# The down projection of a SwiGLU trunk by seven products of halves, its factors made beside gate and up

## The chip, the cores and the metric

The kernel runs on one core of one Trainium2 chip, as one program and one launch. The metric is the time of an execution on the device in microseconds. The kernel before was timed three times: 2983.25 us median, 2979.05 to 2986.69.

## The reference

Two layers of one trunk are computed in fp32 for 1024 latent tokens and 256 context tokens of width 1024. Each layer has a mixer (three kinds of heads between one input and one output projection) and a SwiGLU FFN. Both are normed before and after and are modulated by a vector of the condition:

```python
h_lat = modulate(rmsnorm(x_lat, n1_pre[l]), mod_l[0], mod_l[1])          # the same for h_ctx
y_lat, y_ctx = hybrid_mixer(h_lat, h_ctx, ..., need_ctx)
x_lat = x_lat + mod_l[2] * rmsnorm(y_lat, n1_post[l])
f_lat = swiglu(modulate(rmsnorm(x_lat, n2_pre[l]), mod_l[3], mod_l[4]), ffn_w_gu[l], ffn_w_down[l])
x_lat = x_lat + mod_l[5] * rmsnorm(f_lat, n2_post[l])                    # x_ctx too, in layer 0 only

def swiglu(h, w_gu, w_down):
    g, u = jnp.split(h @ w_gu, 2, axis=-1)
    return (jax.nn.silu(g) * u) @ w_down
```

The FFN is 2816 wide: `w_gu` is 1024 x 5632, `w_down` 2816 x 1024. The context of the last layer has no FFN. The modulation vectors are products of the condition with `mod_w`, six of 1024 a layer.

## The kernel before

Tokens come in ten tiles of 128: 0 and 1 are the context, 2 to 9 the latents. The hidden units of the FFN come in 22 chunks of 128. Every fp32 operand of a large product is split in two fp32r parts, high and low: `halve` lets ScalarE make the high part by a cast and VectorE the low part by a subtraction. `mm3` (L325) then issues three matmuls, high by high, high by low and low by high.

A layer is a row of stages: input projection, mixers, output projection, gate and up of the latents, gate and up of the context (layer 0 only), down. In the profiled execution, in us from the span's start, gate and up of layer 0 run from 758 to 1240, the context's from 1240 to 1372, down to 1703; the projection of layer 1 follows. Gate and up of layer 1 end at 2722, down at 2965, the program at 2978.5.

Gate and up of the latents (class `Up`) already go by seven products for each chunk. The left factors a11, a12, a22 and s1 to s4 are quarters of the latents' normed activations, and sums of quarters; they are made once and stay. The right factors b11, b21, b22 and t1 to t4 are quarters of a chunk's gate and up weights and their differences: `diff` makes the t on GpSimd, `prepare` halves all seven. A chunk has 84 matmuls of 128x512. `head` runs the first two products, `tail` the other five, and between them the results are copied out of the accumulators by ScalarE (L210, L226, L229) or added by VectorE (L213, L242, L249). Silu of gate times up is made on GpSimd (L250, L260), and GpSimd issues the stores to `gd`, four of 128 rows of 2 KB a chunk (L221). The context's 256 tokens follow in `up_context`, with one store of 128 rows a chunk.

Down (`down_stage`) loads `gd` and `w_down` again, halves both, and goes through two halves of five token tiles each (layer 1: of four). For each half the chunks come in groups of two or four. A group runs, for each tile, its chunks by two column halves by three matmuls of 128x512 (L1130) and adds the result to the sums `ya` (L1137). At the last group `post` norms each tile, multiplies by the gate, adds the residual and stores. In layer 0 the next projection's first five tiles are normed and transposed too (`normed`, L547 to L561): one after each group of the second half, the last one after the stage.

The order on each engine: instructions run in the order of their queue. That order is made by a scheduler from the order of emission, and `net.order(a, b)` fixes one pair. SyncE issues the loads. Beside the FFN of layer 0 the modulation vectors are made by VectorE: `mod_stream` yields pieces, each a few 128x512 multiply-adds to `macc` (L523, L525) over a weight tile `ms`. `paced` counts the cost that the main stream yields and advances `mod_stream` by one piece for every 5.6 (gate and up) or 5.2 (down) of it.

## Time and profile before

| | us |
|---|---|
| three runs, median (lowest to highest) | 2983.25 (2979.05 to 2986.69) |
| the profiled execution | 2980.31 |
| its span, first to last instruction | 2978.5 |
| TensorE busy | 2785.4 |
| VectorE busy | 1902.6 |
| ScalarE busy | 1353.1 |
| GpSimd busy | 705.9 |
| mean granted clock of TensorE | 0.965 of 2.4 GHz |

The profile is of one execution. Busy times are of an engine's own instructions. An engine that waits is shown with what ended its wait. A matmul record is longer than the distance to the next one, as matmuls overlap: so a price for a matmul is taken from a stretch's busy time divided by its count. Views used below: windows (busy time of each engine in a stretch), waits of one engine grouped by what ended them, lines (groups of instructions of one line and shape), and the timeline of an engine.

### The profile page before, as it was taken

How to read it: one execution, taken by the hardware profiler on the slowest of the kernel's cores; microseconds unless marked ns; L12 is line 12 of the kernel's file. 1: busy time of each engine (PE TensorE's matmuls, PEld its weight loads, DVE VectorE, ACT ScalarE, POOL GpSimd, SP SyncE). 2: the span in 40 equal slices, each digit the busy share in tenths (PEclk: the TensorE clock that was granted, in tenths of full speed). 3: DMA queues.
4: the chain of work that ended last, by engine and by line, in shares of the span. 5: the costliest groups of instructions: out<-in, count | busy, mean ns of one | idle time of the engine just before them, and what ended most of it. 6: DMA issues, size and time to landing. Idle time of an engine off the chain costs nothing. (4 is left out here: it accounts for less than half of the span.)

```text
span 2978.5 us, 43813 instructions
## 1 busy us (share of the span) xinstructions
PE 2785.4 (94%) x16296; PEld 2373.5 (80%) x16296; DVE 1902.6 (64%) x3640; ACT 1353.1 (45%) x2796; POOL 705.9 (24%) x596
## 2 busy tenths in 40 slices
PE   6999899979899989999999889999888999999998
PEld 4999788868677768898888789888776788887886
DVE  3465578866685994446888664788857443344565
ACT  4454577645433323444242255477645433334331
POOL 0000233310345445200000000043402555552000
PEclk8999789989999999999999999999988999999999
DMA  7743000065453432576665344200164322224552
GB/s 237 222 137 98 24 12 9 13 199 185 142 187 102 139 106 83 166 220 205 194 226 177 109 130 115 72 5 12 54 213 151 97 85 85 82 67 168 165 198 85
DMA packets 339809, 370.45 MB, mean 124 GB/s; under 512 B 45440, under 2 KB 261516, under 8 KB 339596
## 3 DMA queue, kind: packets, MB, share of 16 engines
q1 hardware_dynamic: 327100, 329.38, 35.7%
q0 software_dynamic: 11776, 35.66, 3.2%
q8 instruction: 128, 2.10, 0.3%
q10 hardware_dynamic: 720, 2.62, 0.2%
q14 instruction: 85, 0.70, 0.1%
HBM read 300.19 MB, written 67.40 MB: 123 GB/s over the span
## 5 line engine op out<-in xcount | busy, mean ns | idle before, releaser
L1130 PE MATMUL b<-wh,g 128*128 128x512 f32 x792 | 218.8, 394 | 9.2 <-ACT g L1458 6.9
L1130 PE MATMUL b<-dh,g 128*128 128x512 f32 x792 | 215.7, 390 | 2.6 <-DVE ya L1137 2.5
L326 PE MATMUL b<-wh,hh 128*128 128x256 f32 (+1 forms) x592 | 173.3, 294 | 21.8 <-DVE hh L560 20.7
L1130 PEld LDWEIGHTS b<-wh,g 128*128 128x128 f32 x792 | 149.2, 189 | 44.2 <-ACT g L1458 8.1
L1130 PEld LDWEIGHTS b<-dh,g 128*128 128x128 f32 x792 | 148.4, 188 | 35.4 <-DVE ya L1137 4.5
L525 DVE SCALAR_TENSOR_TENSOR macc<-ms,csil,macc 128x512 f32<-128x512 f32 x196 | 175.4, 935 | 0.9 <-DMA ms<-in_mod_w 0.9
L326 PE MATMUL b<-wh,hl 128*128 128x256 f32 (+1 forms) x592 | 171.4, 290 | 1.3 <-DVE hl L561 1.2
L634 DVE TENSOR_TENSOR wl<-ws,wh 128x1024 fp32r<-128x1024 f32 (+2 forms) x68 | 79.8, 1176 | 145.0 <-ACT wh L633 145.0
L326 PE MATMUL b<-wl,hh 128*128 128x256 f32 (+1 forms) x592 | 171.6, 290 | 0.5 <-DVE wl L634 0.5
L1137 DVE TENSOR_TENSOR ya<-ya,b 128x512 f32<-128x512 f32 x180 | 116.1, 681 | 84.0 <-PE b L1130 83.7
L326 PE MATMUL b<-hh,wh 128*128 128x320 f32 (+1 forms) x472 | 149.0, 316 | 0.0
L326 PE MATMUL b<-hl,wh 128*128 128x320 f32 (+1 forms) x472 | 147.2, 312 | 0.0
L326 PE MATMUL b<-hh,wl 128*128 128x320 f32 (+1 forms) x472 | 146.9, 311 | 0.0
L326 PEld LDWEIGHTS b<-wh,hh 128*128 128x128 f32 x592 | 114.3, 193 | 25.6 <-ACT code L692 17.2
L1056 DVE TENSOR_TENSOR ptl<-b,pth 128x640 fp32r<-128x640 f32 (+2 forms) x144 | 107.4, 746 | 34.5 <-ACT pth L1055 33.1
L633 ACT CAST wh<-ws 128x1024 fp32r<-128x1024 f32 (+2 forms) x68 | 68.7, 1012 | 128.3 <-PE b L326 89.2
L1055 ACT CAST pth<-b 128x640 fp32r<-128x640 f32 (+2 forms) x144 | 90.9, 631 | 76.0 <-PE b L1050 75.1
L1130 PE MATMUL b<-wl,g 128*128 128x512 f32 x396 | 123.8, 392 | 0.1
L1130 PE MATMUL b<-dl,g 128*128 128x512 f32 x396 | 122.4, 389 | 0.0
L1037 DVE CUSTOM_DVE_ANT_0 pe<-b,swm,sink 128x640 f32<-128x640 f32 (+1 forms) x128 | 108.0, 845 | 12.8 <-PE b L1032 12.3
L326 PEld LDWEIGHTS b<-wh,hl 128*128 128x128 f32 x592 | 114.3, 193 | 2.0 <-DVE hl L561 2.0
L326 PEld LDWEIGHTS b<-wl,hh 128*128 128x128 f32 x592 | 114.5, 193 | 0.7 <-DVE wl L634 0.7
(386 smaller groups left out, 8528.5 us busy)
## 6 DMA issues: line engine op xcount, KB each, us to landing
ws<-in_ffn_w_down SPq DMA_DIRECT2D x88, 512.0 KB, 4.0
ms<-in_mod_w SPq DMA_DIRECT2D x144, 256.0 KB, 3.2
rg<-in_ffn_w_gu SPq DMA_DIRECT2D x66, 512.0 KB, 4.0
ru<-in_ffn_w_gu SPq DMA_DIRECT2D x66, 512.0 KB, 3.8
ws<-in_w_in SPq DMA_DIRECT2D x56, 512.0 KB, 4.8
gd<-ct POOLq DMA_DIRECT2D x88, 256.0 KB, 2.9
gr<-gd SPq DMA_DIRECT2D x44, 320.0 KB, 4.0
gr<-gd SPq DMA_DIRECT2D x44, 256.0 KB, 3.8
```

The lines of the kernel that those rows point to most:

```text
L326: mm = lambda x, y, **kw: self.nc.tensor.matmul(out, x, y, skip_group_check=more, **kw)
L525: nc.vector.scalar_tensor_tensor(x, st, c, x, op0=ALU.mult, op1=ALU.add)
L633: nc.scalar.copy(h[:, : kk * nn], st[:, : kk * nn])
L634: nc.vector.tensor_sub(lo[:, : kk * nn], st[:, : kk * nn], h[:, : kk * nn].bitcast(F32))
L1037: nc.vector.tensor_tensor_reduce(out=p, in0=sc, in1=b["mask"], scale=1.0, scalar=sink, op0=ALU.add, op1=ALU.min, accum_out=mn)
L1055: nc.scalar.copy(hi, pv)
L1056: nc.vector.tensor_sub(lo, pv, hi.bitcast(F32))
L1130: nc.tensor.matmul(ps[n], x[:, s], y[:, n * 512 : (n + 1) * 512], start=(c == 0 and pi == 0), stop=(c == nk - 1 and pi == 2))
L1137: nc.vector.tensor_add(y, y, ps[n])
```

## The change

A product of two matrices of 2x2 blocks has eight products of blocks. The change computes down with seven, for each pair of token tiles: (0, 1) in layer 0, and (2, 6), (3, 7), (4, 8), (5, 9). The rows of a block matrix are the two tiles, the columns are the chunks c and c + 11; `w_down` is cut in the same rows and in its two column halves. So T = 5 pairs in layer 0, 4 in layer 1.

- Gate and up goes through its chunks in the order 0, 11, 1, 12, ... After the second of a pair, `factors` makes s1 to s4 from the four results (four operations, VectorE for the latents, GpSimd for the context) and stores seven factors to `gx`, each 128 rows by 4 tiles by 128 (the context: one tile). After the first of a pair, `differences` loads two chunks of `w_down`, makes four differences in place (two on VectorE, two on GpSimd) and stores them to `td`.
- `prepare` can be ordered after the copy of an accumulator, and t3, b22 and t4 of a chunk are halved in its own head.
- `down_stage` runs seven products p, each over all pairs t: a step (p, t) is 11 chunks by three matmuls into one accumulator. Results are added into `ya` and `yb`. Product 5 finishes the first tile of a pair, product 6 the second; from the second step of product 6 on two of the next projection's tiles are normed a step. A step costs 7.5 for `paced`, with 4.4 a piece.
- Staging of the modulation has four buffers beside gate and up in place of eight. In layer 0 the context's tile 1 is normed whole before the tails begin.

```diff
+    def factors(self, pool, j, w, vector):
+
+        nc = self.nc
+        g, at, n = self.g, self.lat if w == 512 else 0, w // P
+        v = lambda x: g[x][:, :w]
+        new = lambda x: g.setdefault(x, self.net.t(pool, f"g{x}", [P, w], bufs=1 if w == 512 else 2))
+        store = lambda x: nc.gpsimd.dma_start(self.gx[:, SUMS.index(x), at : at + n, j, :], v(x).rearrange("p (t n) -> p t n", n=P))
+        new("s1"), new("s2"), new("s4")
+        vector.tensor_add(v("s1"), v("s3"), v("a22"))
+        vector.tensor_sub(v("s2"), v("s1"), v("a11"))
+        vector.tensor_sub(v("s3"), v("a11"), v("s3"))
+        vector.tensor_sub(v("s4"), v("a12"), v("s2"))
+        for x in SUMS:
+            store(x)
+        g.clear()
+
+    def differences(self, pool, j):
+
+        nc, w = self.nc, self.net.a["ffn_w_down"]
+        t = self.net.t(pool, "td", [P, 4, 512], bufs=1)
+        for r in range(2):
+            c = j + KF * r
+            nc.sync.dma_start(t[:, 2 * r : 2 * r + 2, :].rearrange("p h n -> p (h n)"), w[self.l, c * P : (c + 1) * P, :])
+        b11, b12, b21, b22 = [t[:, x, :] for x in range(4)]
+        nc.vector.tensor_sub(b11, b12, b11)
+        nc.gpsimd.tensor_sub(b12, b22, b12)
+        nc.vector.tensor_sub(b22, b22, b11)
+        nc.gpsimd.tensor_sub(b21, b22, b21)
+        nc.sync.dma_start(self.td[:, :, j, :], t)
...
-    def prepare(self, c, x):
-        self.net.halve(*self.slot(c, x), self.raw[c, x])
+    def prepare(self, c, x, after=None):
+        r = self.net.halve(*self.slot(c, x), self.raw[c, x])
+        if after is not None:
+            self.net.order(r, after)
 
     def product(self, out, c, x, y, first=False):
...
         self.product(X, c, "b11", "a11", True)
         p1 = self.tmp()
-        nc.scalar.copy(p1, X)
+        copied = nc.scalar.copy(p1, X)
+        if c > 1:
+            for x in ("t3", "b22", "t4"):
+                self.prepare(c, x, copied)
         self.product(Y, c, "b21", "a12", True)
         g0 = self.tmp()
...
         p5 = self.tmp()
-        nc.scalar.copy(p5, Z)
+        copied = nc.scalar.copy(p5, Z)
         if 1 < n < NFC:
-            self.prepare(n, "b11")
-            self.prepare(n, "b21")
+            self.prepare(n, "b11", copied)
+            self.prepare(n, "b21", copied)
         if more:
             self.diff(n, "t1")
             self.diff(n, "t2")
@@ -241,27 +295,29 @@
...
+            self.prepare(n, "t1", freed)
+            self.prepare(n, "t2", freed)
         yield 2.7
         self.product(Z, c, "b22", "s4")
         c12 = self.tmp()
...
             self.diff(n, "t3")
-            self.prepare(n, "b22")
-            self.prepare(n, "t3")
         yield 2.7
         self.product(X, c, "t4", "a22")
         g1 = self.tmp()
         net.act(g1, X, AF.Silu)
-        nc.gpsimd.tensor_mul(g1, g1, c22)
-        store(768, g1)
+        nc.gpsimd.tensor_mul(mine(("s3", "a22")[r]), g1, c22)
         if more:
             self.diff(n, "t4")
-            self.prepare(n, "t4")
+        if n == 1:
+            for x in ("t3", "b22", "t4"):
+                self.prepare(1, x)
+        if r:
+            self.factors(self.sg, j, 512, nc.vector)
+        else:
+            self.differences(self.sg, j)
...
-                    if need_ctx:
-                        next(rest)
-                        for _ in range(8):
-                            next(st)
                     for _ in rest:
                         pass
-                with tp("mb", "left") as mb:
+
+                with tp("sg", "left") as up.sg:
+                    for x in SUMS:
+                        self.t(up.sg, f"g{x}", [P, 512], bufs=1)
+                    self.t(up.sg, "td", [P, 4, 512], bufs=1)
                     if need_ctx:
-
-                        self.mring = mb, 8
+                        self.mring = up.sg, 4
                         self.back = self.mod_stream("dve", [(0, 5)] + [(l + 1, j) for j in (1, 0, 2)])
                     self.paced(st, 5.6)
                     for _ in self.back:
@@ -1265,7 +1264,7 @@
             if need_ctx:
                 self.mring = dn, 3
                 self.back = self.mod_stream("dve", [(l + 1, j) for j in (3, 4, 5)])
-            self.paced(self.down_stage(l, dn, need_ctx, up.gd), 5.2)
+            self.paced(self.down_stage(l, dn, need_ctx, up), 4.4)
...
+    def down_stage(self, l, dn, need_ctx, up):
...
+        def weight(p, j):
+
+            c, n = 2 * j, min(2, KF - 2 * j)
+            if p % 2 and j < 5:
+                h, lo = [x.rearrange("p k t -> p (k t)")[:, j * D : (j + 1) * D] for x in self.H]
+            else:
+                pool, xs = (dn, ("dl", "dh")) if p % 2 == 0 and j < 4 else (self.wp, ("wl", "wh"))
+                lo, h = [self.t(pool, x, [P, D], F32R, bufs=4) for x in xs]
+            t = self.t(self.wp, "ws", [P, D], bufs=2)[:, : n * 512]
+            nc.sync.dma_start(t.rearrange("p (c n) -> p c n", c=n), source(p, c, n))
+            self.halve(h[:, : n * 512], lo[:, : n * 512], t)
+            return [(h[:, q * 512 : (q + 1) * 512], lo[:, q * 512 : (q + 1) * 512]) for q in range(n)]
+
+        def acts(p, t):
+            h, lo = [self.t(dn, f"a{x}", [P, KF, P], F32R, bufs=2) for x in "hl"]
+            for c0, c1 in ((0, 6), (6, KF)):
+                raw = self.t(dn, "ar", [P, 6, P], bufs=2)[:, : c1 - c0]
+                nc.sync.dma_start(raw, up.gx[:, p, t, c0:c1, :])
+                self.halve(h[:, c0:c1], lo[:, c0:c1], raw)
             return h, lo
 
...
+        lo_, hi_ = slice(0, 512), slice(512, D)
+        for n, (p, t) in enumerate(seq):
+            k = n - p * T
+            if k == 0:
+                cur, ahead = W.pop(), []
+            ah, al = nexta
+            if n + 1 < len(seq):
+                nexta = acts(*seq[n + 1])
+            if p < 6:
+                for j in range(6 * k // T, 6 * (k + 1) // T):
+                    ahead += weight(p + 1, j)
+            if k == T - 1:
+                W.append(ahead)
+            ps = self.b1()
+            for c in range(KF):
+                self.mm3(ps, ah[:, c, :], al[:, c, :], cur[c][0], cur[c][1], c == 0, c == KF - 1)
+            A0, A1, B0, B1 = ya[t][:, lo_], ya[t][:, hi_], yb[t][:, lo_], yb[t][:, hi_]
+            if p == 0:
+                nc.scalar.copy(B0, ps)
+            elif p == 1:
+                nc.vector.tensor_add(A0, B0, ps)
+                square(A0, half[:, t, 0:1])
+            elif p == 2:
+                nc.vector.tensor_add(B0, B0, ps)
+            elif p == 3:
+                nc.vector.tensor_add(A1, B0, ps)
+            elif p == 4:
+                nc.vector.tensor_add(B0, B0, ps)
+                nc.vector.tensor_add(B1, A1, ps)
+                square(B1, half[:, T + t, 0:1])
+            elif p == 5:
+                nc.vector.tensor_add(A1, A1, ps)
+                finish(pairs[t][0], ya[t], hi_, half[:, t, :], False)
+            else:
+                nc.vector.tensor_sub(B0, B0, ps)
+                finish(pairs[t][1], yb[t], lo_, half[:, T + t, :], final)
+                if k == 1 and nxt:
                     self.plan(l + 1)
-            cur = ahead
+                for _ in range(2 if k else 0):
+                    if nxt:
+                        nxt.pop(0)()
+            yield 7.5
         for f in nxt:
             f()
 
```

The context's changed chunk, in `up_context`, multiplies silu by up for each of the two tiles apart and calls `up.factors(cu, j, P, nc.gpsimd)` after the second chunk of a pair. `finish` takes the place of `post`: it sums the squares of the two halves of a row, and norms, multiplies and adds as before.

The order on TensorE at the start of gate and up of layer 0: head 1, then s2 by t2 of chunk 0 (names: left factor, right factor, each with h or l for its part; `ht` is the normed context tile 1, `ident` the identity for a transpose). Before:

```order
L326 MATMUL b_1568_8490<-s2h_7109,t2l_8467 128x512
L326 MATMUL b_1604_8646<-s1h_7111,t1h_8460 128x512
...
L326 MATMUL b_1604_8646<-s1h_7111,t1l_8461 128x512
L326 MATMUL b_1652_8892<-a11h_7105,b11h_8785 128x512
...
L326 MATMUL b_1652_8892<-a11h_7105,b11l_8786 128x512
L326 MATMUL b_1653_8893<-a12h_7107,b21h_8789 128x512
...
L326 MATMUL b_1653_8893<-a12h_7107,b21l_8790 128x512
L326 MATMUL b_1568_8490<-s3h_8452,t3h_8472 128x512
...
L1307 MATMUL b_1651_8870<-ident_67,ht_8627 128x128 x4
```

After:

```order
L382 MATMUL b_1568_8470<-s2h_7109,t2l_8447 128x512
L382 MATMUL b_1568_8470<-s3h_8432,t3h_8452 128x512
L1306 MATMUL b_1605_8627<-ident_67,ht_8607 128x128 x4
L382 MATMUL b_1614_8657<-s1h_7111,t1h_8440 128x512
...
L382 MATMUL b_1614_8657<-s1l_7112,t1h_8440 128x512
L1306 MATMUL b_1605_8627<-ident_67,ht_8607 128x128 x4
L382 MATMUL b_1614_8657<-s1h_7111,t1l_8441 128x512
...
L382 MATMUL b_1614_8657<-s1h_7111,t1l_8441 128x512
L382 MATMUL b_1568_8470<-s3l_8433,t3h_8452 128x512
...
L382 MATMUL b_1576_8508<-s2h_7109,t2h_8711 128x512
```

Both transposes of the context tile moved from 133 rows behind s2 by t2 to the second and eighth row behind it, and head 2 (a11 by b11, a12 by b21) no longer stands before the third product.

The order on VectorE in one chunk of gate and up of layer 0, from c12 (L249 before, L303 after) to the next head's sum (L213 before, L266 after). `macc`, which is named `xt` after the change, holds the modulation's sums; ga and gs are the blocks a and s. Before:

```order
L249 TENSOR_TENSOR ct_10188<-b_1911_10091,ct_10108 128x512
L1459 TENSOR_TENSOR b22l_10195<-ru_10094,b22h_10194 128x512
L525 SCALAR_TENSOR_TENSOR macc_10147<-ms_9835,csil_150,macc_10147 128x512
L525 SCALAR_TENSOR_TENSOR macc_10147<-ms_9887,csil_150,macc_10147 128x512 x2
L1459 TENSOR_TENSOR t4l_10221<-tt_10218,t4h_10220 128x512
L525 SCALAR_TENSOR_TENSOR macc_10147<-ms_9930,csil_150,macc_10147 128x512 x2
L525 SCALAR_TENSOR_TENSOR macc_10147<-ms_9979,csil_150,macc_10147 128x512
L1459 TENSOR_TENSOR b11l_10290<-rg_10257,b11h_10289 128x512
L525 SCALAR_TENSOR_TENSOR macc_10147<-ms_9979,csil_150,macc_10147 128x512
L525 SCALAR_TENSOR_TENSOR macc_10147<-ms_10033,csil_150,macc_10147 128x512
L213 TENSOR_TENSOR ct_10254<-b_1943_10227,ct_10240 128x512
```

After:

```order
L303 TENSOR_TENSOR ct_9932<-b_1880_9843,ct_9860 128x512
L504 STREAM_TRANSPOSE ht_9977<-xt_9564 128x512 x2
L184 TENSOR_TENSOR gs_1904_9956<-gs_1866_9785,ga_1902_9952 128x512
L505 TENSOR_REDUCE modr_9555<-ht_9977 128x32
L185 TENSOR_TENSOR gs_1905_9957<-gs_1904_9956,ga_1861_9754 128x512
L186 TENSOR_TENSOR gs_1866_9785<-ga_1861_9754,gs_1866_9785 128x512
L187 TENSOR_TENSOR gs_1906_9958<-ga_1899_9934,gs_1905_9957 128x512
L1458 TENSOR_TENSOR t3l_10001<-tt_9936,t3h_10000 128x512
L1458 TENSOR_TENSOR b22l_10005<-ru_9846,b22h_10004 128x512
L1458 TENSOR_TENSOR t4l_10009<-tt_9954,t4h_10008 128x512
L266 TENSOR_TENSOR ct_10024<-b_1913_9985,ct_9998 128x512
```

The four factors (L184 to L187) stand directly behind c12, and the halves t3l, b22l and t4l of the next chunk behind them, where before the same chunk's t4l and the next chunk's b11l stood.

The order on TensorE at the end of down of layer 0 (`xt` is a normed tile of the next projection; L1130 and L382 down's matmuls, L326 and L382 with 128x288 the projection's). Before:

```order
L1130 MATMUL b_2995_16051<-wh_15707,g_15712 128x512
L547 MATMUL b_2997_16081<-ident_67,xt_16078 128x128 x8
L1130 MATMUL b_3008_16122<-dh_15897,g_15902 128x512
...
L1130 MATMUL b_3040_16260<-dh_15908,g_15913 128x512
L547 MATMUL b_3059_16330<-ident_67,xt_16327 128x128 x8
L326 MATMUL b_3085_16397<-wh_16104,hh_13615 128x288
```

After:

```order
L382 MATMUL b_3160_16429<-dl_15733,ah_16302 128x512
L605 MATMUL b_3132_16259<-ident_67,xt_16256 128x128 x8
L605 MATMUL b_3135_16282<-ident_67,xt_16279 128x128 x8
L382 MATMUL b_3160_16429<-dh_15734,al_16303 128x512
...
L605 MATMUL b_3151_16376<-ident_67,xt_16373 128x128 x8
...
L605 MATMUL b_3154_16399<-ident_67,xt_16396 128x128 x8
L382 MATMUL b_3172_16513<-dh_15651,al_16420 128x512
...
L382 MATMUL b_3172_16513<-wh_16000,al_16420 128x512
L382 MATMUL b_3205_16621<-wh_16220,hh_14043 128x288
...
L382 MATMUL b_3206_16648<-wl_16221,hh_14043 128x288
L605 MATMUL b_3170_16493<-ident_67,xt_16490 128x128 x8
L382 MATMUL b_3206_16648<-wh_16220,hl_14044 128x288
```

The last tile's transposes moved from before the projection's first matmul to behind its first 32.

## Rows read from the trace of the kernel before

**Rows 1.** The page: busy us of each engine (share of the span), instructions.

```profile
PE 2785.4 (94%) x16296; PEld 2373.5 (80%) x16296; DVE 1902.6 (64%) x3640; ACT 1353.1 (45%) x2796; POOL 705.9 (24%) x596
```

**Rows 2.** Stage windows: us; busy us and count by engine, clock, DMA share, GB/s.

```profile
758.00:1240.00 482.00, 443.73 (x1892) 354.51 (x1892) 337.24 (x433) 177.39 (x322) 222.02 (x176) 0.97 0.40 120
1240.00:1372.00 132.00, 126.78 (x1055) 126.58 (x1055) 63.96 (x69) 56.82 (x72) 14.43 (x25) 1.00 0.70 213
1372.00:1540.00 168.00, 165.62 (x720) 135.12 (x721) 138.57 (x221) 57.23 (x79) 0.00 (x0) 0.98 0.64 210
...
2300.00:2722.00 422.00, 415.44 (x1806) 337.78 (x1804) 174.63 (x224) 161.90 (x288) 214.88 (x172) 1.00 0.26 81
2722.00:2965.00 243.00, 241.14 (x1056) 197.49 (x1056) 147.89 (x243) 83.40 (x116) 0.58 (x1) 1.00 0.48 163
```

**Rows 3.** Windows within gate and up of layer 0.

```profile
806.00:902.00 96.00, 86.45 (x362) 68.42 (x361) 79.27 (x97) 36.54 (x68) 45.99 (x37) 0.96 0.51 161
902.00:998.00 96.00, 94.95 (x421) 77.10 (x420) 58.35 (x73) 35.52 (x65) 50.08 (x40) 1.00 0.35 103
998.00:1094.00 96.00, 81.54 (x342) 64.02 (x341) 95.97 (x117) 27.92 (x51) 40.49 (x32) 0.96 0.46 139
1094.00:1240.00 146.00, 143.21 (x631) 116.03 (x629) 67.28 (x88) 53.96 (x95) 67.28 (x55) 0.99 0.28 85
```

**Rows 4.** Waits of TensorE, 755 to 1240: us in total, times, longest.

```profile
PE b L326 <- ACT ct L226: 16.9, 9, 3.1
PE b L326 <- ACT ct L210: 6.9, 4, 3.2
```

**Rows 5.** Timeline of TensorE, 782 to 796: start, us, instruction, [idle before].

```profile
783.48 0.39 PE L326 MATMUL b<-s1h,t1h 128*128 128x512 f32 x1
...
793.20 0.51 PE L326 MATMUL b<-s3h,t3h 128*128 128x512 f32 x1 [1.33 <-ACT s3h L1458]
```

**Rows 6.** Timeline of VectorE, same stretch.

```profile
792.11 0.75 DVE L1358 TENSOR_SCALAR ht<-z,rs_o 128x1024 f32<-128x1024 f32 x1
793.18 0.69 DVE L1459 TENSOR_TENSOR s3l<-tt,s3h 128x512 fp32r<-128x512 f32 x1 [0.32 <-ACT s3h L1458]
```

**Rows 7.** Tile t1l, 760 to 1235: ns min/median/max, first and last start.

```profile
L1459 DVE TENSOR_TENSOR t1l<-tt,t1h x22: 641/688/1773, 768.5 to 1211.4; 128x512 fp32r<-128x512 f32 x22
```

**Rows 8.** VectorE by line, 760 to 1235: busy us, mean ns, idle before.

```profile
L525 DVE SCALAR_TENSOR_TENSOR macc<-ms,csil,macc 128x512 f32<-128x512 f32 x112 | 115.6, 1077 | 0.0
```

**Rows 9.** Timeline of VectorE, 1019 to 1046.

```profile
1020.54 2.06 DVE L525 SCALAR_TENSOR_TENSOR macc<-ms,csil,macc 128x512 f32<-128x512 f32 x3
...
1032.46 4.64 DVE L525 SCALAR_TENSOR_TENSOR macc<-ms,csil,macc 128x512 f32<-128x512 f32 x3
```

**Rows 10.** Timeline of GpSimd, 1026 to 1046.

```profile
1032.08 1.61 POOL L250 TENSOR_TENSOR ct<-ct,ct 128x512 f32<-128x512 f32 x1 [4.87 <-ACT b11h L1458]
```

**Rows 11.** GpSimd by line, whole span.

```profile
L221 POOL DMA_DIRECT2D gd<-ct x88 | 51.3, 583 | 29.1 <-POOL ct L250 14.8 <-POOL ct L260 12.8 <-DMA ru<-in_ffn_w_gu 1.2
...
L1616 POOL DMA_DIRECT2D uv<-in_gdi x2 | 1.7, 860 | 393.1 <-DVE ht L742 225.9 <-DVE sv L787 167.2
```

**Rows 12.** VectorE by line, 1372 to 1710.

```profile
L1137 DVE TENSOR_TENSOR ya<-ya,b 128x512 f32<-128x512 f32 x100 | 64.6, 681 | 31.2 <-PE b L1130 30.9
...
L1459 DVE TENSOR_TENSOR g<-gr,g 128x640 fp32r<-128x640 f32 x44 | 35.9, 819 | 6.1 <-ACT g L1458 5.9
L1459 DVE TENSOR_TENSOR dl<-ws,dh 128x1024 fp32r<-128x1024 f32 x22 | 26.8, 1222 | 10.9 <-ACT dh L1458 7.3 <-DMA gd<-sg 3.5
```

**Rows 13.** The page, DMA issues: count, KB each, median us to landing.

```profile
ws<-in_ffn_w_down SPq DMA_DIRECT2D x88, 512.0 KB, 4.0
```

**Rows 14.** ScalarE by line, 1372 to 1710.

```profile
L1458 ACT CAST dh<-ws 128x1024 fp32r<-128x1024 f32 x20 | 21.0, 1051 | 71.4 <-PE b L1130 54.8 <-DMA ws<-in_ffn_w_down 16.6
```

**Rows 15.** Waits of TensorE, 1360 to 1400.

```profile
PE b L1130 <- ACT g L1458: 4.4, 1, 4.4
```

**Rows 16.** Waits of TensorE, 1400 to 1750.

```profile
PE b L326 <- DVE hh L560: 17.0, 1, 17.0
```

More of the change, by code (lines that the diff above doesn't have):

```diff
@@ new lines, in down_stage, with gates @@
+        W = [sum((weight(0, j) for j in range(6)), [])]
+        nexta = acts(*seq[0])
+        ya, yb = [[self.t(dn, f"y{x}{t}", [P, D]) for t in range(T)] for x in "ab"]
+        half = self.t(dn, "sq", [P, 2 * T, 2])
+        gate = {}
+        def gates(m):
+            if m not in gate:
+                gate.clear()
+                gate[m] = self.t(dn, "gate", [P, D], bufs=1)
+                nc.sync.dma_start(gate[m], self.gdr[l, 5][m : m + 1, :].to_broadcast([P, D]))
+            return gate[m]
```

177 lines of the change are left out of this document (61 added, 116 removed).

## The prediction

> **What bounds the kernel now.** I read the page's busy shares first, then the spans of the stages that the change touches, then in those stages the waits of TensorE, then what the waited-for engine does there. TensorE is busy for 94% of the span [rows 1], so matmuls taken away shorten the time wherever nothing else is nearly as full. The stages differ in this [rows 2]. Gate and up of layer 1 is TensorE's: 415 of 422 us, VectorE 175. Down of layer 1 is TensorE's too: 241 of 243, VectorE 148. In down of layer 0 VectorE is second with 139 of 168 us in the first part, 82%. In gate and up of layer 0 the two alternate: TensorE 444 and VectorE 337 of 482. There the smaller windows tell more [rows 3]: in 998 to 1094 VectorE works without a pause (95.97 of 96 us) and TensorE loses 14.5 us; from 806 to 902 VectorE has 17 us free, from 902 to 998 38, after 1094 it is half idle. TensorE's longest waits there name ScalarE's evacuation copies L226 and L210, 24 us in 13 waits [rows 4]; ScalarE is not full, it stands in its queue behind casts whose input comes late from the full VectorE and from GpSimd.
>
> **The products taken away: -67.9 us.** All down products are 128x512 matmuls at L1130: 10 tiles x 22 chunks x 2 halves x 3 products = 1320 in layer 0, 1056 for 8 tiles in layer 1. After the change a step is 33 of them (11 chunks, three products each); layer 0 has 7x5 steps, 1155 matmuls, layer 1 7x4, 924. 297 go. In layer 1, where nothing interrupts, 1056 take 241.14 us, 228.4 ns each [rows 2]; 297 x 0.2284 = 67.9 us (37.7 in layer 0, 30.2 in layer 1). This assumes that both stages stay TensorE's; the following terms are what speaks against it.
>
> **The start of gate and up in layer 0: +8 us.** Before, TensorE has head 2 and its s1 product to run between the tails' first product and the third one: 36 matmuls, begun at 783.48 [rows 5]. The order of the changed kernel puts the transposes of context tile 1 (ident,ht) there, after one matmul of s3, and moves head 2 far back. Their input, ht of L1358, is ready at 792.9 (a 0.75 us operation begun at 792.11) and the last s3l of the quarters is only begun at 793.18 [rows 6]. So TensorE stands from about 783.5 to about 793, where before it lost 1.33 [rows 5]: 36 x 0.2284 = 8.2 us of cover gone. The bounds are 0 (the chain of tile 1 is brought forward with its transposes) and 12.
>
> **Sums and differences on VectorE: +10 us in layer 0, 0 in layer 1.** Each of 11 pairs of chunks gets four 512-wide adds (s1 to s4) and two differences of weights: 66 operations a layer. A subtraction of this size takes 0.69 us by its median, 1.77 at most [rows 7]; with the median, and with the stage's mean of 1.08 for the pieces of the modulation [rows 8], 66 cost 46 to 71 us. In layer 1 VectorE has 247 us free in the stage: nothing, though s1 waits for GpSimd's product a22, and the halves t3, b22 and t4 of the next chunk are queued behind it; these are wanted 19.2 us later (84 matmuls), so they have the time. In layer 0 the order shows where the work lands: up to the end of the first run of modulation pieces 173 VectorE operations instead of 134, in the second run as many as before. The 39 more, at 0.82 us (95.97 us for 117 operations [rows 3]), are 32 us, against 17 us free in 806 to 902 and some 5 of the 38 after it that the pieces can still reach: 10 us are left. Bounds: -24 (the copies that TensorE waits for no longer stand behind casts, since those are now ordered after them, and all of [rows 4] goes) and +32. I take +10 since 998 to 1094 shows that a full VectorE sets the pace by itself, in whatever order ScalarE works.
>
> In this place the trace shows a second price: three pieces take 2.06 us when GpSimd is idle and 4.64 when its 1.61 us product begins beside them [rows 9, 10]. The Trainium skill ("GPSIMD Engine Reference", section Specifications) says that GpSimd's SBUF interface is shared with VectorE, with contention for VectorE instructions of two SBUF inputs. The change adds exactly such ones on both engines. By that rule the 66 operations would cost the upper 71 us and more; the trace agrees with it in these rows.
>
> **GpSimd: nothing, by the nearest row.** It issues 77 stores a layer in place of 44, each with 512 runs of 512 bytes in place of 128 of 2 KB. The store of 128 runs takes 583 ns to issue, a gather of 256 rows 860 [rows 11]; 277 ns for 128 more gives 0.58 + 3 x 0.28 = 1.4 us for 512 (an estimate), and if everything scaled with the runs 2.33. In layer 1 GpSimd has 214.9 of 422 us busy [rows 2]; without the 43 old stores (25.1) and with 22 differences at 1.61 [rows 10] (35.4) there are 197 us for 77 stores, so it becomes the bound from 2.56 us a store. I take 1.4: hidden. The Trainium skill ("DMA: Bandwidth & Descriptors", the section on the anatomy of one DMA) says that many descriptors can be emitted before the cost shows; by that the store would stay near 0.58, against which the 860 ns row speaks. Hidden in either case.
>
> The context stage runs at 127 of 132 us on TensorE [rows 2]; its sums and stores go to GpSimd, which is busy 14 us there: nothing.
>
> **The opening of down: +3 in layer 0, +8 in layer 1.** The first step needs all six weight tiles within 7.5 us (33 x 0.2284); before, the first group needed two for 60 matmuls, 13.7 us. There are still two staging buffers. A round of two takes the landing (4.0 us), a cast (1.05) and a subtraction (1.22) [rows 12 to 14]: two more rounds after the first are 12.6 us, and the last two chunks' 1.4 us: 14.0, 6.5 more than the step. In layer 0 a wait of 4.4 us of this opening for activations [rows 15] can go: 2.1 to 6.5, I take 3. In layer 1 the second half of every first-step operand holds the last pair of chunks, which is stored and read back only after the last product: GpSimd's product 1.6, issue 1.4, landing and load each up to the 4.0 of the weights, halving 1.5, 12.5 us, with 4.1 us of matmuls (18) to fill it: 8.4. The late weights lie beside it; I take 8. Bounds for both together 0 and 16.
>
> **VectorE in down of layer 0: +8 us.** Additions fall from 100 to 35 (65 x 0.68 = 44 us less [rows 12]); halving grows from 22 weights of 1024 twice and 44 operands of 640, 73 thousand columns, to 77 half weights of 512 and 35 operands of 1408, 89 thousand (1.2 ns each by [rows 12]: 18 us more). Over the stage VectorE is eased, but the pieces of the modulation all fall into products 0 to 2: a step there has two halves of an operand (1.7 us), 1.2 weights (1.5), a sum (0.7), 5 pieces at 0.69 unhindered [rows 9] (3.4) and transposes: 7.3 to 8.5 us against 7.54 of TensorE. 15 steps, half a microsecond each. Bounds 0 and 20.
>
> **The transition to layer 1: -7 us.** Now TensorE stands 17.0 us for hh, tile 4 being normed last [rows 16]. After the change its transposes come after the first 32 projection matmuls and the four other tiles' within the last product. A part of the wait stays, because finish, norm and halving of the next operands together are some 50 us of VectorE in the last five steps' 37.7: 12 of which stay late at the end. Bounds -15 and +3. **The tail** of layer 1 (13.5 us from 2965 to the span's end) has one tile less to finish in a row: -2.
>
> **The sum:** -67.9 + 8 + 10 + 3 + 8 + 8 - 7 - 2 = -39.9. The profiled execution took 2980.31 us (span 2978.5): 2940.4. The median of the three runs is 2983.25, 2.9 above it: **2943 us**.
>
> **Rivals.**
> - Almost all is kept: VectorE's extra work falls into its free time (79 us after 1094) and the evacuation copies come promptly. Then -67.9 + 8 - 24 + 13 - 9 = -79.9 (the start as forecast, the waits of [rows 4] gone, the openings 11 and 2 for the rest of down, transition and tail -9): 2903. For it: TensorE's named waits are for copies [rows 4]; against it: VectorE at 95.97 of 96.
> - Layer 0 gives nothing: VectorE sets gate/up and down there, as it nearly does now, with its upper prices (+32 and +16 in place of 10 and 8), 30 us more: 2973. For it: the 4.64 us rows; against it: layer 0's sums in down fall by 44 us.
> - Slower: GpSimd's store issue costs much more than its rows suggest. It is the bound of layer 1 from 2.56 us, of layer 0 (232 of 482 us without stores) from 3.25. 77 x (X - 2.56) + 77 x (X - 3.25) eats the 40 us from X = 3.2; at 3.5 it is 92 us: 2983 - 40 + 92 = 3035. For it: no row has 512 runs; against it: even 4 times the row of 128 runs is 2.33.
> - It doesn't do what it says: normed tiles stay late and TensorE waits 17 us or more at the transition. That moves only +7 to +10: 2952, within the forecast's own range.
>
> **How the numbers follow.** Forecast (with the last rival) 0.57, almost all kept 0.18, layer 0 gives nothing 0.16, store issue 0.09. About 0.3%, 9 us, can be told from no change, so 2974 to 2992 is the same. Slower takes the 0.09 and a little of the third case, 0.10; same is a third of that case, 0.07; faster 0.83. The range goes from 2903 to 2980, and leaves out the slow rival and a part beyond either end. The likeliest case alone: 2925 to 2962.
>
> **What would show it.** Right: L382 (the new line of all three-product matmuls) holds 297 fewer 128x512 matmuls at 228 ns; a stall of TensorE near 784 us for ht or s3l; VectorE full in more windows between 800 and 1100; store issues of 1 to 2 us; down of layer 1 near 222 us with its loss in the first step; a wait for hh of 5 to 12 us. Wrong: GpSimd above 95% in gate and up of layer 1, TensorE's waits in gate and up of layer 0 gone altogether, or TensorE below 90% in products 3 to 6.

## The result, and the profile after

The changed kernel takes 3019.65 us (median of four runs, 3014.74 to 3024.85), the kernel before 2984.63 with a fourth run: 1.0121 times as long, 95% interval 1.0096 to 1.0145. The forecast was 2943, range 2903 to 2980. The profiled execution has a span of 3022.5 us, 44.0 above the 2978.5 of before.

The page's busy shares, the row that answers to [rows 1]:

```profile
PE 2758.8 (91%) x15999; PEld 2340.4 (77%) x15999; DVE 2008.8 (66%) x3729; ACT 1370.7 (45%) x2839; POOL 899.7 (30%) x805
```

The 297 matmuls are gone (15999 in place of 16296), but TensorE is busy only 27 us less, not 68, and idle 71 us more. The stages, as in [rows 2] (us, then busy us and count of TensorE, its weight loads, VectorE, ScalarE, GpSimd; granted clock, DMA share, GB/s):

```profile
758.00:1297.00 539.00, 457.84 (x1906) 362.37 (x1904) 396.36 (x504) 180.39 (x326) 296.95 (x233) 0.94 0.56 171
...
1430.00:1730.50 300.50, 278.07 (x1211) 223.73 (x1212) 243.82 (x411) 117.47 (x181) 3.96 (x6) 0.95 0.72 236
2307.00:2793.00 486.00, 440.53 (x1859) 354.43 (x1857) 274.80 (x324) 178.57 (x325) 291.47 (x237) 0.96 0.48 147
2793.00:3012.00 219.00, 216.33 (x923) 176.09 (x924) 139.15 (x224) 89.19 (x130) 0.00 (x0) 0.98 0.64 216
```

Measured from the first matmul of a stage to the first of the next one, in us. A wait for a stage's first matmul so counts to the stretch ahead of it, and the forecast's terms for the opening of down (+3 and +8) stand in the rows of gate and up:

| stretch | before | after | difference | forecast |
|---|---|---|---|---|
| up to gate and up of layer 0 | 758.0 | 761.0 | +3 | 0 |
| gate and up of layer 0, latents and context | 614.0 | 669.5 | +55.5 | +21 |
| down of layer 0 to gate and up of layer 1 | 900.7 | 876.6 | -24.1 | -36.7 |
| gate and up of layer 1 | 449.3 | 486.2 | +36.9 | +8 |
| down of layer 1 and tail | 256.5 | 229.2 | -27.3 | -32.2 |

Of 69 us that were to be saved from down on, 51 were. The loss is in gate and up, 92 us, where 29 were forecast. Layer 1 has no modulation beside it and shows the loss alone. Before, the same stretch was:

```profile
2272.70:2722.00 449.30, 430.50 (x1860) 349.12 (x1858) 197.91 (x257) 178.82 (x324) 227.63 (x181) 0.98 0.28 88
```

Two windows split the stage after the change (columns as above):

```profile
2403.00:2523.00 120.00, 103.11 (x416) 82.15 (x415) 68.88 (x73) 36.28 (x65) 77.81 (x60) 0.93 0.64 208
2571.00:2691.00 120.00, 120.00 (x525) 98.38 (x525) 60.37 (x75) 44.17 (x80) 73.10 (x61) 1.00 0.36 101
```

From 2403 to 2523 TensorE loses 17 of 120 us, and its granted clock is 0.93 in the mean, between the levels of 1.2 and 2.4 GHz; from 2571 to 2691 it loses nothing at 1.00, with the same halves, the same sums and the same stores a chunk. What ends in between are the differences of the down weights: GpSimd's last is at 2514.9. The order had put them into the first half of either stage, one in nearly every chunk. In layer 0 they run to 1111 and TensorE is full from 1118 on; but there VectorE's pieces of the modulation end at about the same time, so that layer does not tell the two apart.

Waits of TensorE in gate and up, us in total, times, longest (layer 0 ahead of the context, then layer 1, then layer 1 before the change), which answer to [rows 4]:

```profile
PE b L382 <- DVE t3l L1458: 25.5, 10, 4.9
PE b L382 <- DVE b11l L1458: 14.3, 7, 4.8
PE b L382 <- ACT gh L1457: 12.3, 1, 12.3
PE b L382 <- ACT ct L260: 11.1, 6, 3.2
PE b L382 <- ACT s3h L1457: 9.4, 1, 9.4
```

```profile
PE b L382 <- DVE b11l L1458: 13.4, 4, 5.0
...
PE b L382 <- DVE t3l L1458: 7.5, 4, 3.3
```

```profile
PE b L326 <- DVE b11l L1459: 1.2, 1, 1.2
```

In layer 0 the waits for evacuation copies fell to 11 us; the new ones are for the halves t3l and b11l. Layer 1's 37 us add up from three parts: some 20 are these waits (20.9 in place of 1.2), 10 are longer matmul times at the lower clock (440.5 us in place of 430.5 for as many matmuls), and 6 are the wait for the first operand of down (8.8 in place of 2.5). Why the halves come late is in VectorE's queue. Its waits in layer 1:

```profile
DVE b11l L1458 <- ACT b11h L1457: 55.2, 12, 5.5
...
DVE td L200 <- DMA td<-in_ffn_w_down: 28.8, 10, 7.6
...
DVE td L202 <- POOL td L201: 11.8, 7, 2.7
```

The longest row is not the cause: in a kernel without the differences (below) it is 96.5 us, and TensorE loses nothing by it. The cause lies in the other two, VectorE's two subtractions of a difference, L200 and L202. One difference on the timeline, VectorE first (start, us, instruction, idle time before it and what ended it), then TensorE, GpSimd and SyncE:

```profile
2509.58 1.27 DVE L200 TENSOR_TENSOR td<-td 128x512 f32<-128x512 f32 x1 [7.61 <-DMA td<-in_ffn_w_down]
2510.77 1.75 DVE L1458 TENSOR_TENSOR b11l<-rg,b11h 128x512 fp32r<-128x512 f32 x1
2512.44 1.76 DVE L1458 TENSOR_TENSOR b21l<-rg,b21h 128x512 fp32r<-128x512 f32 x1
2514.12 0.68 DVE L202 TENSOR_TENSOR td<-td 128x512 f32<-128x512 f32 x1
```

```profile
2512.57 0.79 PE L382 MATMUL b<-a11h,b11l 128*128 128x512 f32 x1 [4.96 <-DVE b11l L1458]
```

```profile
2507.69 1.26 POOL L224 TENSOR_TENSOR tt<-ru,rg 128x512 f32<-128x512 f32 x1 [7.48 <-DMA ru<-in_ffn_w_gu]
...
2511.93 1.72 POOL L201 TENSOR_TENSOR td<-td 128x512 f32<-128x512 f32 x1
2514.88 1.67 POOL L203 TENSOR_TENSOR td<-td 128x512 f32<-128x512 f32 x1 [1.23 <-DVE td L202]
```

```profile
2500.24 0.52 SPq L204 DMA_DIRECT2D td<-td  x1
...
2505.84 0.82 SPq L198 DMA_DIRECT2D td<-in_ffn_w_down  x2
2516.58 0.52 SPq L204 DMA_DIRECT2D td<-td  x1
```

SyncE issues the load of two chunks of `w_down` at 2505.84, after the store of the last difference has landed. VectorE stands at L200 from 2501.97 to 2509.58 for it; b11l and b21l, which the next head needs, are queued behind and take 1.75 us each beside GpSimd's operations, where a subtraction of this size without one beside it takes 0.68. TensorE waits 4.96 us for that b11l. GpSimd's L201 stands behind t1 to t3 of the next chunk, and in 7 of 11 differences VectorE's L202 waits for it (not in this one); GpSimd's L203 waits for L202, and SyncE's store for L203. So three in-order queues wait for each other once a chunk, with the work of TensorE's next products behind each of them. SyncE's part of it in layer 1:

```profile
SPq L204 <- POOL td L203: 56.2, 11, 6.5
...
SPq L198 <- DMA td<-td: 32.1, 9, 5.2
SPq L204 <- DMA td<-in_ffn_w_down: 26.6, 9, 5.7
```

At the context's start TensorE waits 12.3 us for gh (above). SyncE's queue shows it: down's first weights L1530 are issued ahead of the context's loads (L1482, L1475) and had waited 27.8 us for their buffers, which TensorE's last products free.

```profile
SPq L1530 <- PE b L382: 27.8, 1, 27.8
```

```profile
1281.24 0.89 SPq L1530 DMA_DIRECT2D ws<-in_ffn_w_down  x2
1282.17 0.94 SPq L1482 DMA_DIRECT2D hc<-hd  x2
```

In down of layer 0 the 17.0 us of [rows 16] are gone, and a wait of 19.0 us stands in their place:

```profile
PE b L522 <- DVE modr L505: 19.0, 1, 19.0
```

GpSimd's store issues, which answer to [rows 11] (ns min/median/max, first and last start; the shortest are the context's, of one tile):

```profile
L182 POOL DMA_DIRECT2D gx<-gs x132: 538/750/773, 837.2 to 2789.9; - x132
...
L182 POOL DMA_DIRECT2D gx<-ga x99: 538/791/813, 811.1 to 2786.8; - x99
```

The factors of four tiles take 0.75 to 0.80 us by their median, against 583 ns for 128 runs and the 1.4 estimated. The row that the estimate started from was misread: L1616 is no gather but a plain load of 256 runs of 2 KB, and a load of the same shape in the kernel before (busy us, mean ns) takes less:

```profile
L1618 POOL DMA_DIRECT2D uv<-in_gdl x2 | 1.5, 734 | 0.0
```

GpSimd is busy 291 of 486 us in layer 1 and no bound.

### The profile page after: what moved, and what is told of

It is laid out like the page before. It is cut to its first block, busy times and chain, and to the rows that moved or that the text cites. A ratio compares the mean times of both kernels' runs of the same rounds, so it can differ in the third digit from the quotient of the medians.

```text
span 3022.5 us, 43657 instructions
## 1 busy us (share of the span) xinstructions
PE 2758.8 (91%) x15999; PEld 2340.4 (77%) x15999; DVE 2008.8 (66%) x3729; ACT 1370.7 (45%) x2839; POOL 899.7 (30%) x805
## 5 line engine op out<-in xcount | busy, mean ns | idle before, releaser
L1457 ACT CAST ah<-ar 128x768 fp32r<-128x768 f32 x126 | 94.0, 780 | 207.7 <-PE b L382 181.4
L382 PE MATMUL b<-wh,hh 128*128 128x256 f32 (+1 forms) x592 | 172.5, 292 | 6.2 <-DVE hh L618 3.8
L382 PE MATMUL b<-wl,hh 128*128 128x256 f32 (+1 forms) x592 | 171.1, 289 | 1.1 <-DVE wl L692 1.1
L382 PE MATMUL b<-wh,hl 128*128 128x256 f32 (+1 forms) x592 | 170.8, 289 | 1.2 <-DVE hl L619 1.2
L382 PE MATMUL b<-hh,wh 128*128 128x320 f32 (+1 forms) x472 | 149.5, 317 | 2.3 <-DVE rs_v L394 2.3
L382 PE MATMUL b<-hl,wh 128*128 128x320 f32 (+1 forms) x472 | 148.0, 314 | 0.8 <-DVE rs_y L396 0.8
L382 PE MATMUL b<-hh,wl 128*128 128x320 f32 (+1 forms) x472 | 147.5, 313 | 0.0
L224 POOL TENSOR_TENSOR tt<-ru,rg 128x512 f32<-128x512 f32 x44 | 65.7, 1493 | 243.9 <-DMA ru<-in_ffn_w_gu 191.3
L382 PE MATMUL b<-dh,ah 128*128 128x512 f32 x288 | 116.1, 404 | 16.4 <-ACT ah L1457 14.6
L382 PEld LDWEIGHTS b<-wh,hh 128*128 128x128 f32 x592 | 113.7, 192 | 10.0 <-issue 5.5
L583 DVE SCALAR_TENSOR_TENSOR xt<-ms,csil,xt 128x512 f32<-128x512 f32 x112 | 119.8, 1118 | 0.0
L1458 DVE TENSOR_TENSOR al<-ar,ah 128x768 fp32r<-128x768 f32 x126 | 107.9, 887 | 15.5 <-ACT ah L1457 15.4
L382 PE MATMUL b<-dh,al 128*128 128x512 f32 x288 | 115.0, 400 | 1.5 <-DVE al L1458 1.5
L382 PE MATMUL b<-dl,ah 128*128 128x512 f32 x288 | 114.9, 400 | 0.6 <-DVE dl L1458 0.6
L382 PEld LDWEIGHTS b<-wl,hh 128*128 128x128 f32 x592 | 113.8, 192 | 1.5 <-DVE wl L692 1.5
```

The costliest lines, as they stand in the source:

```text
L224: self.nc.gpsimd.tensor_sub(v, self.raw[c, p], self.raw[c, q])
L382: mm = lambda x, y, **kw: self.nc.tensor.matmul(out, x, y, skip_group_check=more, **kw)
L583: nc.vector.scalar_tensor_tensor(x, st, c, x, op0=ALU.mult, op1=ALU.add)
L1457: r = self.nc.scalar.copy(h, v)
L1458: self.nc.vector.tensor_sub(lo, v, h.bitcast(F32))
```

## The experiments

All times are medians beside runs of the kernel before on the same chip (2980.4 to 2981.8 us). The changed kernel's own four runs spread over 10 us, so differences from it of 5 to 9 us are hardly clear of that. Stages from first matmul to first matmul, in us:

| kernel | time | gate/up layer 0 | down layer 0 | gate/up layer 1 |
|---|---|---|---|---|
| before | 2984.6 | 480.8 | 313.8 | 449.3 |
| changed | 3019.7 | 535.3 | 299.8 | 486.2 |
| no differences | 2945.5 | 497.3 | 298.1 | 453.9 |
| halvings placed as before | 3040.6 | 550.3 | 297.5 | 495.5 |
| differences late, stored by GpSimd | 2964.4 | 508.4 | 298.7 | 456.3 |
| differences late, stored by SyncE | 2972.9 | 514.3 | 297.7 | 464.6 |
| two buffers in layer 1 | 3018.0 | 535.3 | 298.0 | 487.4 |
| only the store by GpSimd | 3028.7 | 541.0 | 297.2 | 493.7 |
| once a pair, loaded late | 3001.2 | 530.9 | 298.6 | 477.7 |
| all four on GpSimd | 3057.8 | 557.5 | 298.9 | 499.5 |
| modulation at 3.6 | 3006.7 | 535.9 | 288.1 | 483.8 |
| context's loads first | 3014.2 | 528.7 | 297.4 | 484.5 |
| three edits | 2947.6 | 499.5 | 285.2 | 455.9 |
| three edits, store by SyncE | 2962.0 | 517.7 | 285.4 | 464.7 |

**Without the differences.**

```diff
-        else:
-            self.differences(self.sg, j)
...
-                return up.td[:, DIFFERENCES.index(x), c : c + n, :]
+                x = "b12"
```

> Leaves out the differences of the down weights (their loads, four subtractions and stores); the four products that need them read plain halves of w_down instead, the same bytes. Theory A (the differences, one a chunk, hold up the in-order queues of SyncE, VectorE and GpSimd): gate and up of layer 1 falls from 486 to 445 to 455 us, that of layer 0 by 25 to 40 us, the time to 2940 to 2960. Theory B (the later halving of t3, b22 and t4 frees the single stage of up weights too late): no stage moves by more than 10 us, the time stays above 3005. Theory C (the seven stores and the sums of factors): gate and up of layer 1 stays above 470.

Measured 2945.5 us, 0.988 of before (0.985 to 0.991). Layer 1's gate and up is back to 454, at the granted clock that it had before, 0.98:

```profile
2262.50:2716.00 453.50, 430.09 (x1859) 350.17 (x1857) 242.60 (x302) 177.41 (x325) 257.11 (x215) 0.98 0.38 107
```

The differences cost 74 us, twice what the whole change lost. The sums, the seven stores and the new places of the halvings cost layer 1 at most 5 us: theory C falls. (That the time is within 3 us of the forecast, which had priced the differences' operations and not their waits, is partly luck; see the next section.)

**The halvings as before.**

```diff
-        copied = nc.scalar.copy(p1, X)
-        if c > 1:
-            for x in ("t3", "b22", "t4"):
-                self.prepare(c, x, copied)
+        nc.scalar.copy(p1, X)
...
+            self.prepare(n, "b22")
+            self.prepare(n, "t3")
```

> Only the places of the halvings are as in the kernel before (b22, t3, t4 in the tail of the chunk ahead, no order after a copy); the differences stay. Theory A: within 15 us of the changed kernel, 3005 to 3035. Theory B: gate and up of layer 1 back to about 450, of layer 0 30 us shorter, time 2945 to 2965.

3040.6 us, slower still by 21, and 6 above what theory A allowed: theory B falls the other way round, and the row says how. In gate and up of layer 0 TensorE waits for the copy L277, which stands behind casts again:

```profile
PE b L379 <- ACT ct L277: 45.7, 11, 7.7
```

So the new places of the halvings and their order after the copies, both undone here, are together a gain that the change has. That fits the mechanism behind the bound of -24 in the prediction; which of the two makes it was not tried.

**Differences late.** Loaded in the tail of the pair's first chunk, subtracted behind the pair's four sums, a chunk later; stored by GpSimd.

```diff
+        if not r:
+            self.fetch(self.sg, j, early)          # the two loads, ordered after the copy `early`
...
-            self.factors(self.sg, j, 512, nc.vector)
-        else:
-            self.differences(self.sg, j)
+            self.differences(j, self.factors(self.sg, j, 512, nc.vector))   # ordered after s4
...
-        nc.sync.dma_start(self.td[:, :, j, :], t)
+        nc.gpsimd.dma_start(self.td[:, :, j, :], t)
```

> The same differences, one a pair of chunks in place of one a chunk: loaded in the first chunk's tail, subtracted after the pair's four sums, stored by GpSimd. Theory A (waits in queues): gate and up of layer 1 445 to 460 us, the time 2945 to 2970. Theory D (the amount: 66 MB more traffic, 44 more subtractions a layer, shared ports): gate and up of layer 1 stays above 475, time above 3005, while the kernel without differences gains.

2964.4 us, 0.994 of before (0.992 to 0.996): 55 of the 74 us come back with every load, subtraction and store in place. Theory D keeps at most 19. Layer 1's stage:

```profile
2277.00:2733.00 456.00, 431.27 (x1858) 350.81 (x1856) 274.88 (x324) 177.49 (x325) 294.14 (x247) 0.97 0.50 155
```

VectorE is as busy as in the changed kernel, 274.88 us against 274.80: its work is the same, and what stands behind its waits is not. This edit does three things at once (fewer in a row, subtractions a chunk behind their loads, the store's queue), so the next ones take them apart.

**Two buffers in layer 1.**

```diff
-        t = self.net.t(pool, "td", [P, 4, 512], bufs=1)
+        t = self.net.t(pool, "td", [P, 4, 512], bufs=1 if self.lat else 2)
```

> In layer 1 alone the differences have two buffers in place of one, so that a load need not wait for the store before it to land. If that wait (SyncE's L198 and, behind it, VectorE's L200) is the loss: gate and up of layer 1 455 to 465 us, time 2995 to 3003. If it is GpSimd's and VectorE's alternation in their queues, or the traffic: 480 us or more, time within 6 us of the changed kernel.

3018.0 us, no change: the stage takes 487 us. The differences only run faster ahead (their last is at 2467 in place of 2515) and VectorE still waits 26.4 us for their loads. A free buffer doesn't help here, where the order sets the operation right behind its load.

**Only the store by GpSimd.**

```diff
-        nc.sync.dma_start(self.td[:, :, j, :], t)
+        nc.gpsimd.dma_start(self.td[:, :, j, :], t)
```

> The changed kernel with the differences where they were, only their store issued by GpSimd, which makes the last of them, and not by SyncE. If it is SyncE's wait for the differences (83 us in layer 1) that holds the gate and up loads back: gate and up of layer 1 455 to 465 us, time 2960 to 2985. If VectorE's and GpSimd's own waits for the differences (L200, L201) are the loss: within 10 us of 3020.

3028.7 us, 9 more. SyncE's 83 us of waits (L204, above) are not the loss by themselves.

**Once a pair, loaded late.**

```diff
-            nc.sync.dma_start(t[:, 2 * r : 2 * r + 2, :]..., w[...])
+            d = nc.sync.dma_start(t[:, 2 * r : 2 * r + 2, :]..., w[...])
+            self.net.order(d, after)               # the copy of t2 by s2 in the pair's first chunk
```

> The changed kernel with one order added: the loads of a pair's differences wait for the first evacuation copy of the pair's own first chunk, so the differences come once in two chunks through the whole stage and no longer once in a chunk through its first half. Place of the subtractions, engines and SyncE's store as in the changed kernel. If the crowding (one difference in every chunk's chain) is the loss: time 2960 to 2975, gate and up of layer 1 455 to 462 us. If it is each difference's own waits, 3 to 4 us apiece wherever they stand: 3005 to 3025.

3001.2 us, between the two ranges: 18 of the 74 us are the crowding. Most of the rest stays. VectorE waits for the load 11 times in layer 1, 6 to 7 us each, with b11l right behind as before:

```profile
DVE td L201 <- DMA td<-in_ffn_w_down: 69.6, 11, 7.2
```

```profile
2540.14 0.69 DVE L201 TENSOR_TENSOR td<-td 128x512 f32<-128x512 f32 x1 [7.02 <-DMA td<-in_ffn_w_down]
2540.75 1.78 DVE L1459 TENSOR_TENSOR b11l<-rg,b11h 128x512 fp32r<-128x512 f32 x1
```

TensorE's wait moves, though. For b11l it waits only once (1.2 us); once a pair it waits for ScalarE's copy L261, which at 2549.69 had itself waited 2.30 us for a sum of VectorE, L304, behind the late halves:

```profile
PE b L383 <- ACT ct L261: 14.5, 10, 2.0
```

**Differences late, stored by SyncE.** The edit of the late differences without the store's move.

> As the kernel with the differences loaded in the pair's first chunk and subtracted after the pair's sums, but their store stays on SyncE. If what counts is that VectorE finds the loaded weights there (69.6 us of waits for that load in layer 1 when only the rate was halved): 2955 to 2972, gate and up of layer 1 453 to 460 us. If the store's move to GpSimd made the gain: 2990 to 3005.

2972.9 us, on the upper edge of what the theory of the load expected; the 465 us of layer 1's stage miss its 453 to 460. It is 28 us less than the kernel with the late loads, at the same rate, with the same engines, the same queue for the store and the loads ordered after the same copy. What moved is the subtractions, to a chunk later and behind the pair's sums. VectorE's wait for the load is not among its waits any more; that for GpSimd's product, ahead of s1, is unchanged and costs TensorE nothing:

```profile
DVE gs L184 <- POOL ga L320: 47.5, 11, 4.4
...
DVE td L209 <- POOL td L208: 2.3, 1, 2.3
```

This last row warns against one reading: a wait in that place need not cost, whatever its length. The move changes both whether VectorE waits for the load and what stands behind the subtractions; which of the two gives the 28 us no run shows.

The store by GpSimd is worth 8.5 us more here, where it costs 9 in the crowded order. The traces show where: at the end of gate and up. There the store of the last pair's difference, which waits for that difference, stands in SyncE's queue ahead of the next stage's loads. TensorE's wait at the opening of down in layer 1, with SyncE's store and with GpSimd's:

```profile
2748.24 0.79 PE L389 MATMUL b<-dh,ah 128*128 128x512 f32 x1 [17.91 <-ACT ah L1464]
```

```profile
2733.20 0.79 PE L389 MATMUL b<-dh,ah 128*128 128x512 f32 x1 [9.45 <-ACT ah L1464]
```

At the context's start in layer 0 it is 20.9 against 12.7 us. Between the start of layer 1's stage and this place TensorE has no wait in either kernel.

**All four on GpSimd.** `nc.vector.tensor_sub` to `nc.gpsimd.tensor_sub` in both of VectorE's lines.

> The changed kernel with all four subtractions of a pair's differences on GpSimd: VectorE neither makes nor waits for one. If VectorE's place in the chain (40 us of waits at L200 and L202 in layer 1, with b11l and t3l behind them) is the loss: gate and up of layer 1 450 to 465 us, time 2965 to 2990. If GpSimd, with t1 to t4 of the next chunk behind the differences, is the loss: it has 3 us more a pair, time 3020 to 3050.

3057.8 us, 38 worse than the changed kernel, and worse than expected of the rival. VectorE's place in the chain alone is not the loss. With VectorE out of it GpSimd waits for the loads (12.1 us in layer 1, 25.9 in layer 0), and t1 to t4 stand behind; VectorE now waits 35.1 us for the halves of t1, in place of 12.0:

```profile
DVE t1l L1458 <- ACT t1h L1457: 35.1, 15, 5.8
```

**Modulation at 3.6.** In the order of the changed kernel the last sum of the modulation (L505) stands behind four finished tiles (L1573) on VectorE; at 3.6 it stands ahead of all of them.

```diff
-            self.paced(self.down_stage(l, dn, need_ctx, up), 4.4)
+            self.paced(self.down_stage(l, dn, need_ctx, up), 3.6)
```

> The changed kernel with a piece of the modulation for every 3.6 of a down step's 7.5 in place of 4.4, so that the last sum of the modulation stands ahead of the tiles' finishing on VectorE and no longer behind four of them. If TensorE's 19.0 us for modr come from that place in VectorE's queue: the wait is gone, down of layer 0 is 10 to 19 us shorter, the time 3001 to 3010. If VectorE is simply too full there: the 19 us return as waits for al or dl in products 0 to 2, the time stays within 5 us of 3020.

3006.7 us, 13 less; down of layer 0 is 11.7 us shorter. The wait for modr fell from 19.0 to 5.3, and no wait took its place:

```profile
PE b L382 <- ACT ah L1457: 5.9, 2, 4.6
PE b L522 <- DVE modr L505: 5.3, 1, 5.3
```

**The context's loads first.**

```diff
+            if p == 0 and need_ctx:
+                self.order(d, up.behind)           # the first loads of the context's stage
```

> The changed kernel, with the first weights of down (L1530) ordered behind the first loads of the context's stage on SyncE; their buffers come free only when TensorE is done with them, 28 us later, and the context's loads stood behind. If that queue place costs the 12.3 us at the context's start: TensorE waits there at most 4 us, the time is 8 to 12 us less, 3008 to 3012. The rival (the context's memory is free only after gate and up, so the loads can't start earlier): no change.

3014.2 us, 5 less, half of what was expected and inside the spread of the changed kernel's runs. The context's loads go out from 1269.73 on, 12 us earlier than in the changed kernel, and the wait falls from 12.3 to 6.6 us in two parts:

```profile
PE b L382 <- ACT gh L1457: 3.5, 1, 3.5
PE b L382 <- DVE cl L1458: 3.1, 1, 3.1
```

**The three edits together.**

> The three edits together: differences once a pair, modulation at 3.6, the context's loads first. If the three losses are apart from one another, they add: 2964 - 19 - 12 = 2933, 2926 to 2942, faster than the kernel before by 1.3 to 1.9%. If freed time is lost again at the next wait: above 2950.

2947.6 us, 0.991 of before (0.988 to 0.993): faster than both kernels, and between the two ranges expected. What the three gave one by one adds up (3019.7 - 55.3 - 13.0 - 5.4 = 2946.0), but not place by place: the edit of the context's loads gives nothing here. From gate and up of layer 0 to down it takes 642.7 us, with the late differences alone 643.4; the wait for gh is shorter, and one for cl stands behind it. The 2933 expected had taken the two smaller waits at their whole length. What TensorE still waits for, from gate and up of layer 0 on:

```profile
PE b L389 <- DVE b11l L1465: 16.3, 8, 3.7
PE b L389 <- DVE t3l L1465: 15.0, 7, 3.2
...
PE b L389 <- DVE cl L1465: 7.7, 1, 7.7
```

> The three edits together, with the differences' store on SyncE. Load-ahead theory: 2940 to 2955, as with the store on GpSimd, within 8 us of 2947.6. If the store on SyncE holds back the gate and up loads: 15 us or more above it.

The same with SyncE's store: 2962.0 us, 14 more; the expected 8 is missed, and the rival's 15 nearly met. The gate and up stages hold it (518 and 465 in place of 500 and 456), again at their ends: TensorE waits 21.3 us at the context's start and 17.9 at the opening of down in layer 1.

## Why the prediction was wrong

- **Sums and differences, +10 and 0: the step that failed.** The words were "In layer 1 VectorE has 247 us free in the stage: nothing". It priced 66 operations by their duration and the engines by their free time. The sums bear that out (454 us without the differences, 449 before). The differences do not: each is a chain of a load, VectorE, GpSimd, VectorE, GpSimd, a store, and stood between the halves of the next chunk on all three queues. VectorE's wait for the load was not looked for, and what stands queued behind a waiting instruction was asked of s1 alone. The differences cost 74 us where 10 had been taken for them and the sums together. By the experiments, 18 of these are their crowding (3001.2), 28 the subtractions' place a chunk behind their loads (2972.9), 8.5 the last stores in SyncE's queue (2964.4); 19 stay even then, and are open.
- **The products taken away, -67.9: right in count, too large in price.** 297 fewer. But 228.4 ns each came from a row at a granted clock of 1.00. In layer 1 the 923 that are left in the row take 216.3 us at 0.98, 234 ns each; in layer 0 they take 274.3 us at 0.95, 238 ns each, where 1320 took 306.7 before. TensorE's time in down's products fell by 57 us, not 68.
- **SyncE's queue** has no term in the sum. The context's loads behind down's weights cost 12.3 us of wait; 5 us came back by their move, no more than the runs' spread.
- **The opening of down: right.** In layer 1 TensorE waits 11 us for ah and dh, 2.5 before; 8 more were taken.
- **The start of gate and up, +8: right.** TensorE waits 9.4 us for s3h there (1.33 before), the transposes of the context's tile standing where the prediction saw them. Taking it back wasn't tried.
- **VectorE in down, +8, and the transition, -7: the waits right in sum, wrong in place.** The 17.0 us wait went whole, and 19.0 us came for modr. It was not a full VectorE in products 0 to 2 (behind the opening there is no wait there) but a place in its queue, behind four tiles' finishing. The -7 does not follow from its own terms either: 12 of 17 us that stay would be -5.
- **GpSimd's issue: hidden, as said;** 0.75 to 0.80 us a store where 1.4 was taken, 0.17 to 0.22 us for 384 more runs. The estimate took a plain load (L1616) for a gather; by the load of the same shape beside it, 734 ns, it would have been 1.0. By the sentence of the Trainium skill ("DMA: Bandwidth & Descriptors", on the anatomy of one DMA) it should have stayed near 0.58; the trace lies nearer to that than to the estimate. The slow rival fell by its mechanism, though its sign came true.
- **Without the differences the total came near the forecast, in part by luck:** 2945.5 against 2943. Down and what follows it saved 52 us from the two layers' stretches, where 69 were forecast; gate and up lost 23, where 29 were. The 2947.6 of the three edits says nothing for the sum: it has two edits that the forecast did not have, and 19 us of the differences that it did not see.

## What to carry to other kernels

An operation added to an engine with free time can cost its wait and not its duration, if it stands right behind its own load in an in-order queue and the next operands of the bounding engine stand behind it: ask for each added load what is queued behind its first reader, on every engine of the chain. VectorE's 47.5 us of waits ahead of s1 cost nothing, since nothing urgent stood behind. In this kernel side work of load, operation, store went best with its operations a whole step behind its load and behind the step's own. Its store belongs on a queue where the last one doesn't stand ahead of the next stage's loads. Where one stage is full in one half and slack in the other with the same work a step, look for what ends in between.

## What the runs showed that was not expected

A store of 512 runs of 512 bytes is issued by GpSimd in 0.75 to 0.80 us, one of 128 runs of 2 KB in 0.58: four times the runs for a third more. A second buffer for the differences changed nothing (3018.0 against 3019.7), since the order lets the work run ahead until it stands behind its load again. And the clock took its share of the loss: from 2403 to 2523, where TensorE had five waits of 1.5 to 5.0 us, the granted clock was 0.93, and from 2571 to 2691, where it had none, 1.00. Over gate and up of layer 1 it was 0.96, and TensorE was busy 440.5 us for 1859 matmuls that took it 430.1 at 0.98 without the differences, so 10 of that stage's 37 us are the clock's.
